# GpSimd's state-space tables in the written order and a step ahead, phasors with scratch of their own, a third modulation buffer, later first slabs of layer 1

## The chip, the cores and the metric

One core of a Trainium2 chip runs the whole program. The metric is device time in microseconds (us), the median of several executions. TensorE does the matrix products, VectorE, ScalarE and GpSimd the elementwise work, and SyncE issues nearly all transfers, in the order of its queue. In the views these are PE, DVE, ACT, POOL and SP (SPq where the queue itself is meant).

## The reference

A trunk of two layers on x (1024 positions by 1024 features, float32). Each layer normalises x, scales and shifts it by a modulation that is computed from a conditioning vector c, runs a mixer, and adds the gated result back:

```
mod = c @ mod_w[layer] + mod_b[layer]        # shift, scale, gate
h   = rms_norm(x, norm_w[layer]) * (1 + scale) + shift
x   = x + gate * mixer(h)
```

Layer 0's mixer projects h to five pieces. Two feed a causal convolution of 31 taps with a LayerNorm and SiLU behind it. One, u, feeds a diagonal complex state-space recurrence in 32 groups of 16 channels with 64 states each (x_t = a x_(t-1) + B u_t, y = Re(C x) + D u), with a GELU and a gated linear unit behind it. Both results are gated, joined and projected back. Layer 1's mixer is a dilated sliding-window attention with 24 heads in three patterns.

## The kernel before

Every float32 product is made of three products of a rounded high and a low part (`mm3`, L229 to L233; `split`, L202 to L212, makes the parts: the high part on ScalarE, the low part on VectorE or GpSimd). A weight piece arrives raw (`wr`, `wrp`, `wrg`, `fr`), is split into `wh` and `wl` (or `whp`, `wlp`, `whg`, `wlg`), and is used for 24 matmuls of 512 columns in each half of the sequence.

Layer 0 is a loop over *steps* t: 42 steps of two halves per weight piece, then 21 steps for the output projection, of which the last eight, p0 to p7, are t = 55 to 62. A table `side`, filled by `at(t, function)`, hangs small work onto the steps: the state-space part, the convolution, LayerNorm, the modulation of layer 1. The work of a step is issued ahead of the step's own matmuls. On VectorE, ScalarE and TensorE the instructions of layer 0 run in the order in which the program writes them (`manual_schedule`, L487). A scheduler that ranks by priority decides the order on GpSimd and on SyncE's queue. Each engine runs its own list strictly in order.

The state-space part runs in four *quarters* j of eight groups (`ssm_quarter`), one generator each, whose parts are hung at t = 4j + 2, 3, 5, 6, 7, 7, 8 and 11. At 4j + 2 come the phasors T (three VectorE instructions, then three on ScalarE; their scratch is TS), seven GpSimd instructions that make the table HC (scratch HT), four small copies into `bbd`, the 16 small matmuls `pk` that read HC and bbd, and a round trip through memory that makes the matrix M. At 4j + 3 come six GpSimd instructions that make G0 and G1 (scratch GS) and their transposes `pgt`; at 4j + 5 the matmuls sr and si, the rotations V and W by T and a scan W; behind that X, the output matmuls `py` and a round trip of Y. HT, G0, G1, GS and TS share one pool of three buffers, "t2". HC has two buffers, and `py` of a quarter is the last to read its HC.

The modulation rows of layer 1 (`mod_rows`) take 64 chunks of weights of 256 KB, two for each of 32 steps, into the two halves of a buffer `mw`; the matmuls are `pr`.

In LayerNorm `ln_center` makes squares `lq`, `ln_var` sums them by the matmul `va` (L598), `ln_rsqrt` and `ln_norm` follow.

At the end `residual` adds the projected half to x (`xr` loaded, x written, squares `xq`), `hidden` makes the first operands h of layer 1, and `first_slabs` (hung at t = 58 as `open_slabs`) loads four weight slabs `fr` of layer 1 and splits them, the low parts on GpSimd. fr uses the pool tag "cv", which has five buffers and is also that of xr, xq and rs.

Of the kernel before, what the change touches and what calls it, by code (L numbers as in the profile page):

```python
# [9 lines left out]
F32 = mybir.dt.float32  # L10
F32R = mybir.dt.float32r
I32 = mybir.dt.int32
AF = mybir.ActivationFunctionType
ALU = mybir.AluOpType
# [5 lines left out]
MAGIC = 12582912.0  # L20
NEG = -1e30
TURN = 6.2831845
# [43 lines left out]
MODR = ((0, 16), (0, 20), (1, 8), (1, 12), (1, 0), (1, 4), (1, 16), (1, 20))  # L66


class Trunk:
# [181 lines left out]
    def mod_rows(self, ps, pr):  # L251

        nc = self.nc
        w = self.u("mw", tag="mw").rearrange("p (i m n) -> p i m n", i=2, m=4)
        crep = self.cb[:, 0:256].rearrange("p (k n) -> p k n", k=8)
        rows = self.cb[:, 256:384]
        p = pr("pr")[:, 0:128]
        for n, (layer, m) in enumerate(MODR):
            for q in range(4):
                for i in range(2):  # L260
                    nc.sync.dma_start(w[:, i], self.I["mod_r"][n, 2 * q + i])
                yield
                for i in range(2):
                    k = 2 * q + i
                    for j in range(4):
                        nc.tensor.matmul(p[32 * j:32 * j + 32], lhsT=crep[:, k], rhs=w[:, i, j], start=(k == 0),  # L266
                                         stop=(k == 7), tile_position=(0, 32 * j))
            nc.scalar.activation(rows, p, AF.Copy)
            self.mod_late = (ps, rows, layer, m)

# [17 lines left out]
    def layer0(self):  # L288
        nc, tc, I = self.nc, self.tc, self.I
        with self.cx0 as cx:  # L290
# [6 lines left out]
            def ps(name, shape=None, tag="ps"):  # L297
                return pp.tile(shape or [128, 512], F32, tag=tag, name=name, bufs={"ps": 3, "pm": 2}[tag])
# [7 lines left out]
            def pc(name):  # L306
                return pp.tile([128, 2, 512], F32, tag="pc", name=name, bufs=1)
# [34 lines left out]
            with tc.tile_pool(name="start", bufs=8) as sp, order:  # L342
# [102 lines left out]
                sh = pc("sh")  # L445
# [35 lines left out]
                for j in (15, 4):  # L481
# [3 lines left out]
            nc.vector.tensor_copy(self.cb[:, 0:256].rearrange("p (k n) -> p k n", k=8),  # L485
                                  self.ccol.unsqueeze(2).to_broadcast([128, 8, 32]))
            cx.enter_context(tc.manual_schedule(engines={mybir.EngineType.DVE, mybir.EngineType.Activation,  # L487
                                                         mybir.EngineType.PE}))


            seq = [15]
# [45 lines left out]
            def at(t, fn, *a):  # L537
                side.setdefault(t, []).append(lambda: fn(*a))
# [2 lines left out]
            conv = [None] * 4  # L541
            at(1, self.rope_tables)
            for j in range(4):
                for t in (2, 3, 5, 6, 7, 7, 8, 11):
                    at(4 * j + t, next, quarter[j], None)
                for t in (8, 9, 10, 12):
                    at(4 * j + t, lambda j: next(conv[j], None), j)
# [62 lines left out]
            for b in range(2):  # L610
                at(25, ln_sum, b)
                t = 27 + 4 * b
                at(t, ln_mean, b)
                at(t, ln_center, b, 0)
                at(t + 1, ln_center, b, 1)
                at(t + 2, ln_var, b)
                at(t + 2, ln_rsqrt, b)
                at(t + 3, ln_norm, b, (0, 1, 2, 3))


            yc = [[None, None] for _ in range(8)]
# [24 lines left out]
            for n in range(8):  # L646
                b, j = divmod(n, 4)
# [39 lines left out]
            for t in range(42):  # L687
                i, h = divmod(t, 2)
# [10 lines left out]
                p = ps(f"p{key}_{h}")  # L699
# [4 lines left out]
                n = len(rh)  # L704
# [51 lines left out]

            for k in range(8):
                at(57 + k // 2, hidden, k)
            at(58, open_slabs)
            done, po = None, {}  # L760
            for i in range(21, len(seq)):
                t, key = i + 21, seq[i]
                m, b = int(key[1]), int(key[0] == "p")
# [24 lines left out]
    def first_slabs(self):  # L788

        nc = self.nc  # L790
        self.w1 = self.ctx.enter_context(self.tc.tile_pool(name="w1", bufs=4, side="right", reuse_waits="tile"))
        self.slabs = {}
        with self.prio(-150000):
            for i in range(4):
                raw = self.u(f"fr{i}", shape=[128, 2, 384], tag="cv")
                nc.sync.dma_start(raw, self.I["wqkv"][0, 0, :, 2 * i:2 * i + 2])
                self.slabs[0, i] = tuple(self.w1.tile([128, 2, 384], F32R, tag=t, name=t) for t in ("wh", "wl"))
                self.split(*self.slabs[0, i], raw, leng="gpsimd")
# [732 lines left out]
    def ssm_quarter(self, j, us, ps, ysg):  # L1531

        nc, S = self.nc, self.S

        def L(name, tag, shape, bufs=1):
            return self.sp.tile(shape, F32, tag=tag, name=name, bufs=bufs)

        gp, v = nc.gpsimd, nc.vector
        qs = slice(4 * j, 4 * j + 4)

        T = L(f"T{j}", "T", [128, 2, 4, 128], 2)
        n = L(f"TS{j}", "t2", [128, 4, 128], 3)
        sh = [128, 4, 128]
        y = T[:, 0]
        v.tensor_tensor(y, self.P["chunk"].unsqueeze(1).to_broadcast(sh), self.t8[:, qs].unsqueeze(2).to_broadcast(sh),
                        op=ALU.mult)
        v.tensor_scalar(n, y, MAGIC, None, ALU.add)
        v.scalar_tensor_tensor(n, n, MAGIC, y, ALU.subtract, ALU.subtract)
        nc.scalar.activation(T[:, 1], n, AF.Sin, scale=-TURN)
        nc.scalar.activation(y, n, AF.Abs)  # L1550
        nc.scalar.activation(y, y, AF.Sin, scale=-TURN, bias=self.quarter)

        sh = [128, 4, 8, 16]
        HC = L(f"HC{j}", "HC", [128, 2, 4, 8, 16], 2)
        tt = L(f"HT{j}", "t2", sh, 3)
# [13 lines left out]
        for i, b in enumerate((self.bbr, self.bbi)):  # L1569
            gp.tensor_copy(bd[0:64, :, i, 0:16], b[0:64, qs])  # L1570
            gp.tensor_copy(bd[64:128, :, i, 16:32], b[64:128, qs])
        pk = ps(f"pk{j}", [128, 128])
        for q in range(4):
            for i in range(2):
                nc.tensor.matmul(pk[32 * q:32 * q + 32], lhsT=bd[:, q, i],
                                 rhs=HC[:, i, q].rearrange("p t h -> p (t h)"), start=(i == 0), stop=(i == 1),
# [8 lines left out]
        for t in range(8):  # L1585
            nc.sync.dma_start(M[t::8], kd[:, :, (7 - t) * 16:(7 - t) * 16 + 128])
        yield

        sh = [128, 4, 16, 8]
        GT = L(f"GT{j}", "GT", [128, 2, 4, 128])  # L1590
        G = [L(f"G{j}{i}", "t2", sh, 3) for i in range(2)]
        tg = L(f"GS{j}", "t2", sh, 3)
        br = self.bbr[:, qs].unsqueeze(3).to_broadcast(sh)
        bi = self.bbi[:, qs].unsqueeze(3).to_broadcast(sh)
        pr7 = self.prr.rearrange("p t g -> p g t")[:, qs].unsqueeze(2).to_broadcast(sh)
        pi7 = self.pir.rearrange("p t g -> p g t")[:, qs].unsqueeze(2).to_broadcast(sh)
        gp.tensor_tensor(G[0], br, pr7, op=ALU.mult)
        gp.tensor_tensor(tg, bi, pi7, op=ALU.mult)
        gp.tensor_tensor(G[0], G[0], tg, op=ALU.subtract)
        gp.tensor_tensor(G[1], br, pi7, op=ALU.mult)  # L1600
        gp.tensor_tensor(tg, bi, pr7, op=ALU.mult)
        gp.tensor_tensor(G[1], G[1], tg, op=ALU.add)
        for i in range(2):
            pg = ps(f"pgt{j}{i}")
            for q in range(4):
                nc.tensor.transpose(pg[:, q * 128:(q + 1) * 128], G[i][:, q].rearrange("p h t -> p (h t)"),
                                    self.ident)
            nc.scalar.activation(GT[:, i], pg.rearrange("p (q n) -> p q n", q=4), AF.Copy)
        yield

        U = us[j]
        sr, si = ps(f"sr{j}"), ps(f"si{j}")
        for g in range(8):
            q, o = g // 2, 64 * (g % 2)
            for i, s in enumerate((sr, si)):
                nc.tensor.matmul(s[o:o + 64, q * 128:(q + 1) * 128], lhsT=GT[:, i, q, o:o + 64], rhs=U[:, g],
                                 start=True, stop=True)
        V = L(f"V{j}", "VW", [128, 2, 4, 128], 2)
        W = L(f"W{j}", "VW", [128, 2, 4, 128], 2)
        c, s = T[:, 0], T[:, 1]  # L1620
        r4 = lambda a: a.rearrange("p (q n) -> p q n", q=4)
# [10 lines left out]
                                     V[:, i, q], 0.0, ALU.mult, ALU.add)  # L1632
        yield
        X = L(f"X{j}", "X", [128, 2, 4, 128])
        gp.memset(X[:, :, :, 0:1], 0.0)
        xs = X[:, :, :, 1:128]
        V, W, c, s = V[:, :, :, 0:127], W[:, :, :, 0:127], c[:, :, 0:127], s[:, :, 0:127]
        v.tensor_tensor(xs[:, 0], W[:, 0], c, op=ALU.mult)
# [9 lines left out]
        for q in range(4):  # L1648
# [3 lines left out]
            for i in range(2):  # L1652
                for b in range(2):
                    o = 64 * b
                    nc.tensor.matmul(d[b], lhsT=HC[o:o + 64, i, q].rearrange("p t h -> p (t h)"),
                                     rhs=X[o:o + 64, i, q], start=False, stop=(i == 1))
# [12 lines left out]
def p_order():  # L1669

    p = np.arange(1024)
    tok = p // 512 * 512 + p // 32 % 4 * 128 + p % 32 * 4 + p // 128 % 4
    n = np.arange(128)
    return tok, n % 32 * 4 + n // 32


def lay_out(inp):
    a = {k: np.asarray(v) for k, v in inp.items()}
    f = np.float32
    tok, loc = p_order()  # L1680
    col = lambda v: np.ascontiguousarray(v.reshape(-1, 128).T)
    pair = lambda v: v.reshape(16, 2, 64, -1).transpose(1, 2, 0, 3).reshape(128, -1)
# [37 lines left out]
    taps = np.zeros((512, 54), f)  # L1720
    taps[:, 7:38] = a["conv_dw_w"][0].T[:, ::-1]
    taps = np.stack([taps[:, 7 - t:47 - t] for t in range(8)], 1)
    w = a["attn_w_in"][0].reshape(8, 128, 10240)
    qkv = w[:, :, :9216].reshape(8, 128, 3, 3, 8, 128).transpose(4, 3, 1, 0, 2, 5)
    pos = a["positions"][0]
    post = pos[tok].reshape(8, 128).T
    tl = lambda w: w.reshape(w.shape[0] // 128, 128, -1, 128).transpose(2, 1, 0, 3)
# [46 lines left out]
```

## Time and profile before

| what | before |
|---|---|
| median of 3 executions | 1764.66 us |
| lowest, highest | 1764.46, 1767.72 us |
| the profiled execution's own time | 1767.46 us |
| its span in the profile | 1765.7 us |
| TensorE busy | 1675.6 us, 95% |
| VectorE, ScalarE, GpSimd busy | 937.0, 618.7, 505.3 us |
| mean granted clock of TensorE | 0.974 |

The span runs from the first to the last instruction; the execution's own time holds some 1.8 us more around it. Layer 0 takes about the first 560 us. TensorE is the busiest engine, so what counts is where it stands still, and where its clock is granted below full speed (1 in the views).

### The profile page before, as it was taken

What the parts mean: (1) busy time and instruction counts of PE and PEld (TensorE: products, weight loads), DVE (VectorE), ACT (ScalarE), POOL (GpSimd) and SP (SyncE); (2) the same over time, 40 slices, a digit from 0 to 9 for tenths busy, and PEclk for the clock granted to TensorE, in tenths of its full rate; (3) what the DMA queues carried; (4) which work ended last, traced back from release to release, by engine and by line L of the source; (5) the groups of instructions that cost most, each with busy time, mean ns of one, the idle gap of its engine ahead of it and who ended that gap; (6) DMA issues with size and microseconds to landing.
All of it is one profiled execution on the core that took longest, in us unless ns stands there. A gap on an engine that the chain in (4) does not pass through costs nothing.

```text
span 1765.7 us, 28609 instructions
## 1 busy us (share of the span) xinstructions
PE 1675.6 (95%) x10520; PEld 1524.2 (86%) x10520; DVE 937.0 (53%) x2332; ACT 618.7 (35%) x1860; POOL 505.3 (29%) x737
## 2 busy tenths in 40 slices
PE   8967779989997999999999999999999999999999
PEld 5755657767776999999999999999999999999887
DVE  8823444344555745654664564565575475465551
ACT  5311322363333433333333333333333333333410
POOL 6234320200014532332332233233233243333000
PEclk8988889999998999999999999999999999999999
DMA  9433445524553201211311211211221221121243
GB/s 353 143 95 90 135 144 160 174 96 138 183 177 98 62 25 55 73 43 41 87 43 35 65 62 29 76 52 34 61 76 34 58 82 37 44 63 61 84 156 102
DMA packets 94189, 159.84 MB, mean 91 GB/s; under 512 B 13281, under 2 KB 43745, under 8 KB 94050
## 3 DMA queue, kind: packets, MB, share of 16 engines
q1 hardware_dynamic: 94050, 158.02, 29.1%
q8 instruction: 83, 1.36, 0.3%
q14 instruction: 56, 0.46, 0.1%
HBM read 130.54 MB, written 23.23 MB: 87 GB/s over the span
## 4 chain that ended last, share of the span: by engine, by line
PE 84%; issue 5%; DVE 3%; POOL 3%; ACT 2%; DMA 1%; SPq 0%; POOLq 0%; ACTq 0%; DVEq 0%
PE pj L233 17%; PE pj L231 17%; PE pj L232 17%; PE O L1142 4%; PE S L1093 4%; PE p L231 4%; PE p L232 3%; PE p L233 3%; PE tqk L1047 2%; PE tP L1120 2%; PE po L233 2%; PE po L231 2%; PE po L232 2%; PE pr L266 1%; DMA mw<-in_mod_r 1%
## 5 line engine op out<-in xcount | busy, mean ns | idle before, releaser
L231 PE MATMUL pj<-wh,h 128*128 128x384 f32 x1536 | 542.9, 353 | 0.0
L233 PE MATMUL pj<-wh,h 128*128 128x384 f32 x1536 | 516.7, 336 | 0.8 <-DVE h L224 0.8
L232 PE MATMUL pj<-wl,h 128*128 128x384 f32 x1536 | 516.0, 336 | 0.0
L231 PEld LDWEIGHTS pj<-wh,h 128*128 128x128 f32 x1536 | 289.1, 188 | 1.1 <-issue 0.2
L232 PEld LDWEIGHTS pj<-wl,h 128*128 128x128 f32 x1536 | 289.7, 189 | 0.3 <-issue 0.2
L233 PEld LDWEIGHTS pj<-wh,h 128*128 128x128 f32 x1536 | 288.3, 188 | 1.4 <-DVE h L224 1.4
L1032 POOL TENSOR_TENSOR B<-u,sin 128x256 f32<-128x256 f32 x192 | 190.3, 991 | 210.6 <-DVE u L1028 210.6
L1004 ACT ACTIVATE sq<-pj 128x128 f32<-128x128 f32 x384 | 103.0, 273 | 351.1 <-PE pj L233 321.2
L212 DVE TENSOR_TENSOR wl<-raw,wh 128x768 fp32r<-128x768 f32 (+1 forms) x124 | 115.9, 949 | 124.5 <-ACT wh L209 123.9
L1005 POOL TENSOR_SCALAR ss<-ss 128x2 f32<-128x2 f32 x192 | 40.8, 212 | 488.4 <-ACT sq L1004 488.2
L1028 DVE SCALAR_TENSOR_TENSOR u<-pj,ss,pk 128x128 f32<-128x128 f32 x384 | 116.3, 344 | 74.7 <-POOL ss L1006 74.6
L1069 DVE COPY qk<-tqk 128x256 f32<-128x256 f32 x188 | 79.0, 420 | 139.5 <-PE tqk L1047 139.5
L1006 POOL TENSOR_TENSOR ss<-ss,mh 128x2 f32<-128x2 f32 x192 | 138.1, 719 | 16.0
L1113 ACT ACTIVATE E<-E,nm 128x256 f32<-128x256 f32 (+2 forms) x128 | 71.3, 557 | 198.7 <-DVE nm L1112 198.7
L231 PE MATMUL p<-h0h,wh 128*128 128x512 f32 x272 | 114.8, 422 | 0.0
L232 PE MATMUL p<-h0l,wh 128*128 128x512 f32 x272 | 110.6, 407 | 0.0
L233 PE MATMUL p<-h0h,wl 128*128 128x512 f32 x272 | 110.0, 404 | 0.0
L209 ACT ACTIVATE wh<-raw 128x768 fp32r<-128x768 f32 (+1 forms) x124 | 97.3, 790 | 28.8 <-PE po L232 15.0
L1040 DVE TENSOR_TENSOR u<-A,B 128x128 f32<-128x128 f32 x192 | 56.2, 293 | 88.4 <-POOL B L1032 81.6
L1039 DVE TENSOR_TENSOR A<-u,cos 128x256 f32<-128x256 f32 x192 | 96.6, 503 | 4.4
L1093 PE MATMUL S<-qk 128*128 128x128 f32 x544 | 86.4, 274 | 0.0
L1093 PEld LDWEIGHTS S<-qk 128*128 128x128 f32 x544 | 80.9, 190 | 1.3
(449 smaller groups left out, 2789.2 us busy)
## 6 DMA issues: line engine op xcount, KB each, us to landing
raw<-in_wqkv SPq DMA_DIRECT2D x92, 384.0 KB
mw<-in_mod_r SPq DMA_DIRECT2D x64, 256.0 KB
wr<-in_w SPq DMA_DIRECT2D x17, 512.0 KB
al<-ad SPq DMA_DIRECT2D x16, 512.0 KB
x<-in_x SPq DMA_DIRECT2D x8, 512.0 KB
mw<-in_scale SPq DMA_DIRECT2D x8, 512.0 KB
mw<-in_shift SPq DMA_DIRECT2D x8, 512.0 KB
xr<-in_xp SPq DMA_DIRECT2D x16, 256.0 KB
```

Source lines behind the costliest of these rows:

```text
L209: nc.scalar.activation(hi, src, AF.Copy)
L212: getattr(nc, leng).tensor_tensor(lo, src, hi.bitcast(F32), op=ALU.subtract)
L231: mm(ps, lhsT=lh, rhs=rh, start=first, stop=False)
L232: mm(ps, lhsT=lh, rhs=rl, start=False, stop=False)
L233: mm(ps, lhsT=ll, rhs=rh, start=False, stop=last)
L1004: sc.activation(sq[:, i], p[:, i * 128:(i + 1) * 128], AF.Square, accum_out=ss[:, i:i + 1])
L1006: gp.tensor_tensor(ss, ss, mh, op=ALU.pow)
L1028: v.scalar_tensor_tensor(u[:, i].rearrange("p a b -> p (a b)"), p[:, i * 128:(i + 1) * 128], ss[:, i:i + 1], w, ALU.mult, ALU.mult)
L1032: gp.tensor_tensor(f(B), f(u), sin[:, ti].unsqueeze(1).to_broadcast([128, 4, 64]), op=ALU.mult)
L1039: v.tensor_tensor(f(A), f(u), cos[:, ti].unsqueeze(1).to_broadcast([128, 4, 64]), op=ALU.mult)
L1069: v.tensor_copy(out, tp)
L1093: pe.matmul(ps[:, i * 128:(i + 1) * 128], lhsT=qT[h, g, t], rhs=kT[h, g, kt], start=True, stop=True)
```

## The change

GpSimd joins the engines in written order. In `ssm_quarter` the tables HC, bbd and G become a first part of their own, at t = 0, 3, 8 and 12; pk, its round trip and M stay at 4j + 2, the transposes at 4j + 3; the phasors move to 4j + 4, and their scratch TS to another pool ("e"). `mod_rows` takes half of the tile cb as a third buffer and asks for chunk c + 3 right behind the matmuls of chunk c. LayerNorm's `ln_var`, `ln_rsqrt` and `ln_norm` come a step later. `open_slabs` moves from t = 58 to 60, and fr from the tag "cv" to the default one. X's small memset moves from GpSimd to VectorE.

```diff
 def mod_rows(self, ps, pr):
     w = self.u("mw", tag="mw").rearrange("p (i m n) -> p i m n", i=2, m=4)
+    w = [w[:, 0], w[:, 1], self.cb[:, 512:1024].rearrange("p (m n) -> p m n", m=4)]
+    def load(c):
+        if c < 8 * len(MODR):
+            nc.sync.dma_start(w[c % 3], self.I["mod_r"][c // 8, c % 8])
+    for c in range(3):
+        load(c)
...
         for q in range(4):
-            for i in range(2):
-                nc.sync.dma_start(w[:, i], self.I["mod_r"][n, 2 * q + i])
             yield
-            for i in range(2):
-                k = 2 * q + i
+            for k in (2 * q, 2 * q + 1):
+                c = 8 * n + k
                 for j in range(4):
-                    nc.tensor.matmul(..., rhs=w[:, i, j], ...)
+                    nc.tensor.matmul(..., rhs=w[c % 3][:, j], ...)
+                load(c + 3)
...
 cx.enter_context(tc.manual_schedule(engines={mybir.EngineType.DVE, mybir.EngineType.Activation,
-                                             mybir.EngineType.PE}))
+                                             mybir.EngineType.PE, mybir.EngineType.Pool}))
...
 for j in range(4):
-    for t in (2, 3, 5, 6, 7, 7, 8, 11):
+    for t in ((0, -1, 0, 0)[j], 2, 3, 4, 5, 6, 7, 7, 8, 11):
         at(4 * j + t, next, quarter[j], None)
...
-    at(t + 2, ln_var, b)
-    at(t + 2, ln_rsqrt, b)
-    at(t + 3, ln_norm, b, (0, 1, 2, 3))
+    at(t + 3, ln_var, b)
+    at(t + 3, ln_rsqrt, b)
+    at(t + 4, ln_norm, b, (0, 1, 2, 3))
...
-at(58, open_slabs)
+at(60, open_slabs)
...
-    raw = self.u(f"fr{i}", shape=[128, 2, 384], tag="cv")
+    raw = self.u(f"fr{i}", shape=[128, 2, 384])
...
 def ssm_quarter(...):
-    (T: scratch TS from "t2"; three VectorE, three ScalarE instructions)
     (HC: seven GpSimd instructions; bbd: four copies)
+    (G0, G1: six GpSimd instructions)
+    yield
     (pk, kp, Kd, M)
     yield
-    (G0, G1: six GpSimd instructions)
     (pgt, GT)
+    yield
+    (T: scratch TS from self.ep, tag "e"; the same six instructions)
     yield
...
-    gp.memset(X[:, :, :, 0:1], 0.0)
+    v.memset(X[:, :, :, 0:1], 0.0)
```

(The lines in parentheses stand for code that is moved unchanged but for the scratch.)

In the order of GpSimd's instructions in quarter 0, in the stretch that ends the table HC, stood before (HC_902, HT_903 and G_964, GS_966 are the tables and scratch of this quarter, 0):

```order
L1561 TENSOR_TENSOR HT_903<-pk,pi 128x512
L1597 TENSOR_TENSOR G_964<-bbr,prr 128x512
L1562 TENSOR_TENSOR HC_902<-HC_902,HT_903 128x512
L1598 TENSOR_TENSOR GS_966<-bbi,pir 128x512
L1564 TENSOR_TENSOR HT_903<-pk,pr 128x512
L1599 TENSOR_TENSOR G_964<-G_964,GS_966 128x512
L1565 TENSOR_TENSOR HC_902<-HC_902,HT_903 128x512
L1601 TENSOR_TENSOR GS_966<-bbi,prr 128x512
L1566 TENSOR_SCALAR HC_902<-HC_902 128x512
L1600 TENSOR_TENSOR G_965<-bbr,pir 128x512
```

and now, from the start of the same quarter's tables:

```order
L1555 TENSOR_TENSOR HC_813<-pk,pr 128x512
L1556 TENSOR_TENSOR HT_814<-pk,pi 128x512
L1557 TENSOR_TENSOR HC_813<-HC_813,HT_814 128x512
L1558 TENSOR_TENSOR HC_813<-pk,pi 128x512
L1559 TENSOR_TENSOR HT_814<-pk,pr 128x512
L1560 TENSOR_TENSOR HC_813<-HC_813,HT_814 128x512
L1561 TENSOR_SCALAR HC_813<-HC_813 128x512
L1565 COPY bbd_781<-bbr 64x4x16
L1566 COPY bbd_781<-bbr 64x4x16
L1565 COPY bbd_781<-bbi 64x4x16
L1566 COPY bbd_781<-bbi 64x4x16
L1575 TENSOR_TENSOR G_826<-bbr,prr 128x512
```

The two tables were interleaved, with GS, which takes a buffer of "t2", ahead of the last three instructions of HC; now HC's seven instructions and the copies stand together, and all of G behind them.

In ScalarE's order at the end of layer 0 (wh<-fr are the high parts of layer 1's slabs, xq the squares of a residual, whp the high part of an output-projection piece, h an operand of layer 1) stood before:

```order
L218 ACTIVATE h_3_0_4065<-x_2_0_3749,mod_0_2847 128x512
L209 ACTIVATE wh<-fr_4075 128x768
L209 ACTIVATE wh<-fr_4081 128x768
L209 ACTIVATE wh<-fr_4087 128x768
L209 ACTIVATE wh<-fr_4093 128x768
L732 ACTIVATE xq_4127<-x_2_1_4049 128x512
L209 ACTIVATE whp_4131<-wrp_3973 128x1024
```

and now:

```order
L218 ACTIVATE h_6_0_4152<-x_6_0_3877,mod_4_3195 128x512
L218 ACTIVATE h_7_0_4156<-x_6_0_3877,mod_4_3195 128x512
L209 ACTIVATE wh<-fr_4166 128x768
L209 ACTIVATE wh<-fr_4172 128x768
L209 ACTIVATE wh<-fr_4178 128x768
L209 ACTIVATE wh<-fr_4184 128x768
L739 ACTIVATE xq_4218<-x_4_1_4142 128x512
L209 ACTIVATE whp_4222<-wrp_4059 128x1024
```

The four slab splits stood ahead of the whp that p5 reads; now they stand ahead of the whp that p7 reads, behind h6 and h7.

## Rows read from the trace of the kernel before

**Rows 1.** Stretches: length; busy PE, PEld, DVE, ACT, POOL; clock; DMA; GB/s.
```profile
72.00:140.00 68.00, 41.47 (x221) 32.23 (x219) 26.16 (x39) 17.39 (x25) 25.84 (x25) 0.81 0.47 147
590.00:1000.00 410.00, 410.00 (x2575) 402.15 (x2574) 224.90 (x655) 149.27 (x569) 135.63 (x214) 1.00 0.19 52
```

**Rows 2.** TensorE's waits, 72 to 600: total us, times, longest.
```profile
PE pk L1575 <- POOL HC L1566: 47.1, 4, 15.1
PE pr L266 <- DMA mw<-in_mod_r: 11.0, 8, 3.2
PE pop L231 <- ACT whp L209: 10.2, 2, 9.4
PE va L598 <- DVE lq L592: 6.0, 3, 3.6
```

**Rows 3.** GpSimd's waits, 66 to 340: total us, times, longest.
```profile
POOL GS L1598 <- ACT T L1550: 76.7, 4, 22.7
...
POOL HC L1560 <- PE py L1655: 34.3, 2, 18.2
```

**Rows 4.** Timeline, GpSimd, quarter 0: start, duration, instruction, wait ahead.
```profile
66.11 1.61 POOL L1560 TENSOR_TENSOR HC<-pk,pr 128x512 f32<-128x512 f32 x1 [24.27 <-ACT h0h L407]
...
69.20 2.09 POOL L1560 TENSOR_TENSOR HC<-pk,pr 128x512 f32<-128x512 f32 x1
...
91.58 1.31 POOL L1598 TENSOR_TENSOR GS<-bbi,pir 128x512 f32<-128x512 f32 x1 [13.70 <-ACT T L1550]
92.85 1.10 POOL L1564 TENSOR_TENSOR HT<-pk,pr 128x512 f32<-128x512 f32 x1
...
97.62 1.50 POOL L1566 TENSOR_SCALAR HC<-HC 128x512 f32<-128x512 f32 x1
```

**Rows 5.** Chain that ended last, quarters 1 and 2: start, duration, piece.
```profile
130.33 1.28 DVE W L1631 x4
...
133.49 0.63 ACT T L1549
...
163.53 0.65 PE py L1655 x8
```

**Rows 6.** Stretches of single steps, columns as in group 1.
```profile
100.20:107.60 7.40, 7.40 (x27) 5.92 (x25) 0.53 (x2) 0.00 (x0) 2.38 (x6) 0.74 0.29 66
153.40:159.00 5.60, 5.60 (x28) 4.56 (x25) 0.00 (x0) 1.54 (x3) 0.00 (x0) 1.00 0.30 97
252.20:258.80 6.60, 6.60 (x27) 5.30 (x25) 6.59 (x11) 0.00 (x0) 2.03 (x2) 0.84 0.35 98
285.00:292.30 7.30, 7.30 (x28) 5.61 (x24) 1.54 (x5) 0.07 (x1) 0.00 (x0) 0.77 0.44 146
538.10:547.50 9.40, 9.32 (x26) 6.64 (x26) 5.71 (x7) 3.58 (x5) 2.40 (x2) 0.66 0.47 149
```

**Rows 7.** Timeline, SyncE's queue, quarter 1: issue time, its length.
```profile
163.56 5.04 SPq L1586 DMA_DIRECT2D M<-Kd  x8
168.71 5.23 SPq L1660 DMA_DIRECT2D Yd<-Y  x8
```

**Rows 8.** Timeline, TensorE: a chunk of modulation weights, and pk of quarter 2.
```profile
176.87 0.43 PE L266 MATMUL pr<-mw,cb 128*32 128x128 f32 x8 [1.76 <-DMA mw<-in_mod_r]
...
195.49 0.67 PE L1575 MATMUL pk<-HC,bbd 128*32 128x128 f32 x8 [9.12 <-POOL HC L1566]
```

**Rows 9.** Timeline, VectorE: one form beside GpSimd and alone.
```profile
68.19 4.17 DVE L212 TENSOR_TENSOR wl<-wr,wh 128x1024 fp32r<-128x1024 f32 x2
...
87.31 1.22 DVE L212 TENSOR_TENSOR wl<-wr,wh 128x1024 fp32r<-128x1024 f32 x1 [2.67 <-ACT wh L209]
```

**Rows 10.** Timeline, VectorE, end of layer 0.
```profile
544.08 0.74 DVE L726 SCALAR_TENSOR_TENSOR x<-pop,mod,xr 128x512 f32<-128x512 f32 x1
...
551.53 0.74 DVE L726 SCALAR_TENSOR_TENSOR x<-pop,mod,xr 128x512 f32<-128x512 f32 x1
```

**Rows 11.** Timeline, ScalarE, end of layer 0.
```profile
534.16 0.84 ACT L209 ACTIVATE wh<-fr 128x768 fp32r<-128x768 f32 x1 [4.46 <-DMA fr<-in_wqkv]
```

More of the change, by code (lines that the diff above doesn't have):

```diff
@@ L259, in mod_rows @@
             for q in range(4):
-                for i in range(2):
-                    nc.sync.dma_start(w[:, i], self.I["mod_r"][n, 2 * q + i])
                 yield
-                for i in range(2):
-                    k = 2 * q + i
+                for k in (2 * q, 2 * q + 1):
+                    c = 8 * n + k
                     for j in range(4):
-                        nc.tensor.matmul(p[32 * j:32 * j + 32], lhsT=crep[:, k], rhs=w[:, i, j], start=(k == 0),
+                        nc.tensor.matmul(p[32 * j:32 * j + 32], lhsT=crep[:, k], rhs=w[c % 3][:, j], start=(k == 0),
                                          stop=(k == 7), tile_position=(0, 32 * j))
+                    load(c + 3)
             nc.scalar.activation(rows, p, AF.Copy)
@@ L1539, in ssm_quarter @@
         qs = slice(4 * j, 4 * j + 4)
[L1541 to L1551, printed above, removed]
         sh = [128, 4, 8, 16]
@@ L1571, in ssm_quarter @@
             gp.tensor_copy(bd[64:128, :, i, 16:32], b[64:128, qs])
+        sh = [128, 4, 16, 8]
+        G = [L(f"G{j}{i}", "t2", sh, 3) for i in range(2)]
+        tg = L(f"GS{j}", "t2", sh, 3)
+        br = self.bbr[:, qs].unsqueeze(3).to_broadcast(sh)
+        bi = self.bbi[:, qs].unsqueeze(3).to_broadcast(sh)
+        pr7 = self.prr.rearrange("p t g -> p g t")[:, qs].unsqueeze(2).to_broadcast(sh)
+        pi7 = self.pir.rearrange("p t g -> p g t")[:, qs].unsqueeze(2).to_broadcast(sh)
+        gp.tensor_tensor(G[0], br, pr7, op=ALU.mult)
+        gp.tensor_tensor(tg, bi, pi7, op=ALU.mult)
+        gp.tensor_tensor(G[0], G[0], tg, op=ALU.subtract)
+        gp.tensor_tensor(G[1], br, pi7, op=ALU.mult)
+        gp.tensor_tensor(tg, bi, pr7, op=ALU.mult)
+        gp.tensor_tensor(G[1], G[1], tg, op=ALU.add)
+        yield
         pk = ps(f"pk{j}", [128, 128])
@@ L1587, in ssm_quarter @@
         yield
-        sh = [128, 4, 16, 8]
         GT = L(f"GT{j}", "GT", [128, 2, 4, 128])
[L1591 to L1602, printed above, removed]
         for i in range(2):
@@ L1608, in ssm_quarter @@
             nc.scalar.activation(GT[:, i], pg.rearrange("p (q n) -> p q n", q=4), AF.Copy)
+        yield
+        T = L(f"T{j}", "T", [128, 2, 4, 128], 2)
+        n = self.ep.tile([128, 512], F32, tag="e", name=f"TS{j}").rearrange("p (q n) -> p q n", q=4)
+        sh = [128, 4, 128]
+        y = T[:, 0]
+        v.tensor_tensor(y, self.P["chunk"].unsqueeze(1).to_broadcast(sh), self.t8[:, qs].unsqueeze(2).to_broadcast(sh),
+                        op=ALU.mult)
+        v.tensor_scalar(n, y, MAGIC, None, ALU.add)
+        v.scalar_tensor_tensor(n, n, MAGIC, y, ALU.subtract, ALU.subtract)
+        nc.scalar.activation(T[:, 1], n, AF.Sin, scale=-TURN)
+        nc.scalar.activation(y, n, AF.Abs)
+        nc.scalar.activation(y, y, AF.Sin, scale=-TURN, bias=self.quarter)
         yield
```

## The prediction

> **What bounds the kernel now.** I read the stretches first. In layer 1 TensorE is busy for all 410.00 of 410 us at clock 1.00; in the first stretch of the state-space quarters it is busy for 41.47 of 68.00 at 0.81 [rows 1]. So this change, which is all in layer 0, can only win there. The list of TensorE's waits says what for: pk, which waits for GpSimd's last HC instruction, 47.1 us in four waits; the modulation matmuls pr, which wait for their weights, 11.0 in eight; an output-projection piece, 10.2; LayerNorm's va, 6.0 [rows 2].
>
> GpSimd itself is not short of time. Its own waits hold 76.7 us ahead of GS, for the ScalarE instruction on the phasors T [rows 3]: GS takes a buffer of "t2" that TS held. The timeline shows it in quarter 0: GS starts at 91.58 after 13.70 us of idling, and HC ends at 99.12 [rows 4], which is when pk can begin. In quarter 1 the chain goes one link further back: T comes behind the W scan on VectorE and ends at 134.1 [rows 5]. Thus T, which nobody needs for three more steps, delays HC, which TensorE needs at once.
>
> A wait costs more than itself. The step right behind pk runs 7.40 us at clock 0.74 in quarter 0 and 6.60 at 0.84 in quarter 3, where an undisturbed one takes 5.60 at 1.00 [rows 6]. That is between the chip's two levels, 1.2 and 2.4 GHz: the step starts low after TensorE stood still and ends high.
>
> **The tables.** Per quarter thirteen GpSimd instructions and four small copies are moved ahead of pk, as the order shows; none is added. What goes is the wait, 47.1 [rows 2], and the slow steps behind it: 7.40 and 6.60 for the first and last, 1.8 and 1.0 over 5.60; the two others I take as like these, in sum 2 x (1.8 + 1.0) = 5.6 [rows 6]. Together 52.7.
>
> Is HC in time everywhere? Quarter 0: HC starts at 66.11. Seven instructions at the 1.61 seen there end at 77.4, at 2.09, the longest seen, at 80.7 [rows 4], and the copies add at most about 1. TensorE arrives at pk 15.1 before 99.2, at 84.1 [rows 2, 4]. Quarters 2 and 3: HC may only be written when py of two quarters before has read its buffer. Before, py of quarter 0 ended at 164.2 [rows 5] and TensorE reached pk of quarter 2 at 195.49 - 9.12 = 186.4 [rows 8]; 22 us less what other waits go in between (1.76 there) still leaves some 19 for 7 x 1.5 + 1 = 11.5, or 15.6 at 2.09. Margins are thus 2 to 8 us. G, the transposes and T have a step and more each. T's six instructions now precede sr, si and V by one step of 5.6 us and more; they take 0.63 to 0.7 us each, some 4, and the slack pays. X's memset on VectorE lies in the time that it waits.
>
> Here the order of engines could hurt. With GpSimd busy, VectorE's split of 128 x 1024 took 4.17 us for two, 2.09 each, with GpSimd idle 1.22 [rows 9]; GpSimd's own instruction took 2.09 against 1.10 [rows 4]. The Trainium skill, "GPSIMD Engine Reference", section 1 (Specifications), says that GpSimd shares its SBUF interfaces with VectorE and that VectorE's instructions with two SBUF inputs contend; the trace agrees (2.09 against 1.10). If every one of the thirteen ran at 2.09, the tables would take 27 us a quarter and VectorE's work beside them 1.7 times its time. VectorE is busy for 26.16 of 68 [rows 1], so the sum is left as it is, and the contention raises the chance of the first rival.
>
> **The modulation weights.** SyncE's queue is in order. In quarter 1, M's eight transfers took 5.04 us to issue and Y's eight 5.23 [rows 7]; the pair of chunks behind them landed late, and pr waited 1.76 for the first [rows 8]. With three buffers the first chunk of a step is asked for a step earlier than now; the second still has one step's lead, since its buffer is free only when the first of the step before has been used. I take half of 11.0, 5.5. Bounds: 3, if the second chunk is what is mostly late; 11.0 and a slow step behind it, 7.30 against 5.60 [rows 6], together 12.7.
>
> **LayerNorm.** va waits 6.0 in three waits, at most 3.6 [rows 2]. A step later is 2.8 us for a half-length step (the gated unit's pieces have half the matmuls) and 5.6 for a full one. I take all 6.0; at worst 4; at best 6.0 and a slow step's 1.7 more [rows 6]. Its consumers, the output projection's operands, come many steps on.
>
> **The slabs.** Now: 10.2 of waiting and a step of 9.40 where 5.60 would do [rows 2, 6], 14.0 in all. It comes from ScalarE, which waited 4.46 for fr ahead of whp [rows 11]; xr stood behind fr in the shared buffers. After: the chain from one residual to the next takes 551.53 - 544.08 = 7.45 on VectorE [rows 10] where TensorE wants 5.60, so p5 and p6 wait 1.85 each, 3.7; and p7's whp now stands behind four wh of 0.84, 3.4 [rows 11], with a slow step, half of the 3.8 above, behind it. The gain is 14.0 - 3.7 - 3.4 - 1.9 = 5.0. Bounds: 0.5 with fr again 4.46 late; 10.6 if the residuals keep up and p7's step stays fast.
>
> **Sum.** 52.7 + 5.5 + 6.0 + 5.0 = 69.2 us. The profiled execution took 1767.46, so the same one would take 1698.3; it stands 2.8 above the median, 1764.66, from which the forecast follows: 1695.5.
>
> **Rivals.** First: HC is still late in quarters 2 and 3, where it follows py and contends with VectorE. For it: 34.3 us of GpSimd's waits are already for py [rows 3], and the margin at 2.09 is 3 us or less. Against: at 1.5 each it is 7. If 9.1 stays in both, with the slow step of 1.0 behind, 20.2 come back: 1716.
>
> Second, on the slower side: SyncE's queue becomes the bound. The loads are now 64 single ones; each waits for the matmuls of the chunk three before, and M, Y, the layer's weights wr and the convolution's reads stand behind it. The waits for pk, which covered such lateness, are gone. For it: pr waits at all, behind 10.3 us of issues [rows 7, 8]. The Trainium skill, "DMA: Bandwidth & Descriptors", section "Anatomy of one DMA — SWDGE (gpsimd) path", says that a transfer's semaphore wait happens on the issuing sequencer before dispatch; by that, everything behind such a load is late with it, and the trace, where pr waits behind Y's issues, agrees so far. It decides from 69.2 / 32 = 2.2 us for each of the 32 modulation steps; at 2.5 each it costs 80 and the time is 1775. Against: the matmuls that a load waits for take 0.43 us for eight [rows 8], just ahead of the step's own 5.60.
>
> Third: T was not what held GS, and pk's wait stays whole, released by something else, such as the transposes that free "t2". Then only the small terms count, 16.5: 1748. Against: the row of GS itself names T's second ScalarE instruction as its releaser, and so does the list for all four quarters [rows 3, 4].
>
> Fourth: the end of layer 0 gives nothing or loses 3, as p7 waits for all four slabs: up to 8 back, 1703, within the range below.
>
> **Chances.** Forecast with its small terms anywhere in their bounds 0.66; first rival 0.19; slabs 0.07; third 0.03; queue 0.03; else, about evenly on both sides, 0.02. The range: best terms 52.7 + 12.7 + 7.7 + 10.6 = 83.7 give 1681, the first rival 1716. A measurement of this kernel tells some 0.2%, 3.5 us, from no change: every case but the queue is beyond it on the faster side. So faster 0.96, the same 0.01, slower 0.03.
>
> **What would show it.** Right: no wait of pk on HC; GpSimd's first wait of a quarter for py or pgt, not for T; clock 1.00 in the steps behind pk; pr's waits halved; va's gone; waits of 1 to 5 us at p5 to p7. Wrong: pk still waiting, with HC's instructions at 2 us; SyncE's M or wr issued behind a modulation load with TensorE waiting for either; a new wait for T's consumers V and W.

## The result and the profile after

The changed kernel takes 1700.06 us, median of 4 executions (1699.71 to 1702.04), against 1765.06 before in the same comparison: a ratio of 0.9631, 95% interval 0.9615 to 0.9648, or 65.0 us less. The forecast was 1695.5 (69.2 less) with a range of 1681 to 1716. The profiled execution took 1702.04 us with a span of 1700.3, at a mean granted clock of 0.991 (0.974 before).

Where the time went is read from five starts in TensorE's timeline: the first projection matmul p, the first matmul pg of the gated linear unit, the first of the output projection (poo0b), the first statistic st inside it, and layer 1's first, pj.

| stretch | before | after | change | forecast |
|---|---|---|---|---|
| p (72.39; 72.03) to pg: state space, convolution, modulation | 287.34 | 231.34 | -56.0 | -58.2 |
| pg (359.73; 303.37) to poo0b: gated unit, LayerNorm, gates | 92.17 | 85.97 | -6.2 | -6.0 |
| poo0b (451.90; 389.34) to st | 52.82 | 52.72 | -0.1 | 0 |
| st (504.72; 442.06) to pj: end of layer 0 | 55.67 | 53.07 | -2.6 | -5.0 |
| pj (560.39; 495.13) to the end: layer 1 | 1205.3 | 1205.2 | -0.1 | 0 |

The first line is the forecast's sum of the tables (52.7) and the modulation weights (5.5). Layer 1 has not moved, so all of it was won in the places that the profile of before named.

TensorE's waits of the changed kernel, 60 to 600 us (total us, times, longest), which answer to [rows 2]:

```profile
PE pop L231 <- ACT whp L209: 4.7, 3, 3.7
PE pgt L1602 <- DVE kp L1589: 4.5, 1, 4.5
PE pr L272 <- DMA mw<-in_mod_r: 4.5, 5, 1.4
PE pop L233 <- DVE wlp L212: 4.0, 4, 2.5
PE va L605 <- DVE lq L599: 3.0, 1, 3.0
PE pr L272 <- DMA cb<-in_mod_r: 1.7, 1, 1.7
```

No wait of pk is left of the 47.1. In its place is one that the forecast did not have: the transposes pgt, 4.5 us, for the VectorE instruction kp. pr is down from 11.0 to 6.2 (4.5 + 1.7), va from 6.0 to 3.0. The end of layer 0 (pop) waits 4.7 + 4.0.

GpSimd's waits, 60 to 340, which answer to [rows 3]:

```profile
POOL ls L585 <- PE pc L830: 78.8, 1, 78.8
POOL HC L1555 <- PE py L1664: 48.2, 2, 26.6
POOL HC L1555 <- ACT h0h L414: 26.4, 1, 26.4
POOL ls L585 <- DVE cv L854: 12.9, 1, 12.9
```

It no longer waits for T at all (ls belongs to the convolution's LayerNorm). HC waits for py, 48.2 us in two waits, as the prediction said it would, and TensorE does not wait for it in turn.

Two stretches as in [rows 1], and two pieces behind waits, as in [rows 6] (the columns are those of group 1):

```profile
72.00:140.00 68.00, 63.46 (x399) 50.25 (x398) 44.03 (x55) 23.51 (x34) 40.15 (x34) 0.95 0.58 179
590.00:1000.00 410.00, 410.00 (x2575) 402.16 (x2574) 233.26 (x667) 148.24 (x568) 136.03 (x213) 1.00 0.19 55
95.50:101.30 5.80, 5.80 (x18) 4.63 (x17) 0.00 (x0) 0.60 (x1) 5.39 (x8) 0.60 0.84 247
190.97:198.30 7.33, 7.33 (x28) 5.56 (x24) 4.16 (x5) 0.13 (x1) 6.51 (x5) 0.77 0.46 165
```

TensorE is busy for 63.46 us of the stretch where it was for 41.47, at clock 0.95 where it was 0.81. The slow steps behind pk are gone. Others stand behind the waits that are left: 0.60 right behind the new wait of pgt, and a step of 7.33 at 0.77 behind a wait of pr.

### The profile page after: what moved, and what is told of

Same layout as the page of the kernel before. It is cut to its first block, busy times and chain, and to the rows that moved or that the text cites. A ratio compares the mean times of both kernels' runs of the same rounds, so it can differ in the third digit from the quotient of the medians.

```text
span 1700.3 us, 28611 instructions
## 1 busy us (share of the span) xinstructions
PE 1663.6 (98%) x10520; PEld 1516.7 (89%) x10520; DVE 952.2 (56%) x2336; ACT 618.9 (36%) x1860; POOL 514.6 (30%) x733
## 4 chain that ended last, share of the span: by engine, by line
PE 83%; issue 5%; DVE 4%; DMA 3%; ACT 2%; SPq 2%; POOL 1%; ACTq 0%; DVEq 0%; POOLq 0%
PE pj L231 17%; PE pj L233 17%; PE pj L232 17%; PE O L1149 4%; PE S L1100 4%; PE p L231 3%; PE p L232 3%; PE p L233 3%; PE tqk L1054 2%; PE tP L1127 2%; PE po L233 2%; PE po L232 2%; PE po L231 2%; DMA mw<-in_mod_r 1%; SPq L1669 1%
```

## The experiments

All are edits of the changed kernel, except where the text says that they are edits of the kernel before. "..." in a diff marks lines that are left out.

**1. The scratch alone.** The kernel before, with TS from the pool of temporaries:

```diff
-        n = L(f"TS{j}", "t2", [128, 4, 128], 3)
+        n = self.ep.tile([128, 512], F32, tag="e", name=f"TS{j}").rearrange("p (q n) -> p q n", q=4)
```

> The kernel before with one edit: the phasors' scratch TS comes from the pool of temporaries instead of the three shared buffers; GpSimd's order stays the scheduler's, and T stays ahead of pk. Theory (the shared buffer was the whole cause of the wait of pk): GS no longer waits for T, pk's waits fall from 47.1 us to under 5, and the time from 1765 to about 1712. Rival (the order of GpSimd is needed too, because G's instructions stand between HC's): half or more of pk's wait stays, 1735 to 1750.

Measured: 1724.9 us (ratio 0.9774, 0.9759 to 0.9788), 40 less with one line. TensorE's waits:

```profile
PE pr L266 <- DMA mw<-in_mod_r: 12.6, 13, 1.8
...
PE pgt L1606 <- DVE kp L1579: 4.1, 1, 4.1
PE pk L1575 <- POOL HC L1566: 3.6, 1, 3.6
```

The wait for pk falls from 47.1 to 3.6, in quarter 0 only. So the shared buffer was its cause, as the theory has it; the time is 13 over the theory's 1712. Waits make up 9.3 of it: pk's 3.6, 4.1 of pgt that it had not waited before, and pr's 12.6 instead of 11.0. Slow steps stand behind all three.

**2. The state-space edit alone.** The kernel before with the whole edit of `ssm_quarter` and its steps (tables first, T later, own scratch), the scheduler still ordering GpSimd:

```diff
-                for t in (2, 3, 5, 6, 7, 7, 8, 11):
+                for t in ((0, -1, 0, 0)[j], 2, 3, 4, 5, 6, 7, 7, 8, 11):
...
```

> The kernel before with the state-space edit alone: the tables as a step of their own, the phasors later and with their own scratch, X's memset on VectorE; the scheduler still orders GpSimd, and modulation, LayerNorm and slabs are as before. Theory (the shared scratch was the cause, the tables' own step is worth nothing more): 1722 to 1727, as with the scratch alone, 1724.9. Rival (the own step removes something besides the wait for T): 1716 to 1720, which is also what comes out if the effects of the other parts, 11, 4 and 3.5 us as measured in the changed kernel, are added to its time with the scheduler's order, 1699.7.

Measured: 1718.45 (0.9740, 0.9726 to 0.9753), in the rival's range: 6.5 less than with the scratch alone, so the moved steps do more than free T's buffer, which this run's theory denied. pk still waits 3.6 here. VectorE's timeline in quarter 0, with the scratch alone:

```profile
93.52 1.62 DVE L212 TENSOR_TENSOR wl<-wr,wh 128x1024 fp32r<-128x1024 f32 x1 [2.67 <-ACT wh L209]
95.06 1.59 DVE L1545 TENSOR_TENSOR T<-pk,t 128x512 f32<-128x512 f32 x1
...
99.69 0.28 DVE L1579 COPY kp<-pk 128x128 f32<-128x128 f32 x1
```

and with the whole state-space edit:

```profile
93.47 1.61 DVE L212 TENSOR_TENSOR wl<-wr,wh 128x1024 fp32r<-128x1024 f32 x1 [2.67 <-ACT wh L209]
95.00 0.28 DVE L1582 COPY kp<-pk 128x128 f32<-128x128 f32 x1
```

With the scratch alone, T's three instructions (the first is shown) stand ahead of kp, which empties pk's accumulator; it comes at 99.69 and the transposes wait for it. With T two steps later kp comes at 95.00, and pgt waits nowhere. That is the 4.1 us and the slow step behind it (8.01 us where an undisturbed one, timed from its first matmul to its last, takes 5.86).

**3. GpSimd's order left to the scheduler.**

```diff
-                                                         mybir.EngineType.PE, mybir.EngineType.Pool}))
+                                                         mybir.EngineType.PE}))
```

> The changed kernel, with GpSimd's order left to the scheduler again; the tables' own step, T's place and its scratch stay. Theory (the written order adds little once TS has its own scratch): GpSimd's list has G's and the next HC's instructions between those of HC, some five of 1.5 to 2 us in quarter 0, so pk waits about 3 us there and little elsewhere: 1700 to 1705. Rival (the written order carries the gain): pk waits 5 to 10 us in each quarter, 1720 to 1745.

Measured: 1699.67 (0.9632, 0.9618 to 0.9647), no difference from 1700.06. But the waits differ:

```profile
PE pk L1585 <- POOL HC L1561: 3.6, 1, 3.6
...
PE pgt L1602 <- DVE kp L1589: 0.2, 1, 0.2
```

pk waits its 3.6 again, as the theory says, and of pgt's 4.5 only 0.2 is left: kp comes at 95.0 us here and at 94.3 in the changed kernel, so TensorE waits for it at the transposes or has waited at pk already. The written order won time that the next late instruction took back.

**4. Two modulation buffers again** (the loop of the kernel before in `mod_rows`, pairs of loads).

> The changed kernel, with the modulation weights asked for in pairs into two buffers again. Theory (the third buffer takes the wait off the first chunk of a step and leaves it on the second): pr's waits go from 6.2 us back to 10 to 12, some slow steps return, the time is 1705 to 1708. Rival (the waits come from the place of the loads in SyncE's queue behind the transfers of M and Y, whatever the number of buffers): pr's waits stay within 1.5 us of 6.2 and the time within 2 us of 1700.

Measured: 1711.24 (0.9695, 0.9679 to 0.9712), 11 more than with three, where the theory gave 5 to 8.

```profile
PE pr L266 <- DMA mw<-in_mod_r: 13.0, 13, 2.0
```

pr waits 13.0, not 6.2, and in TensorE's timeline three steps of 7.41 us, against 5.87 undisturbed, stand behind these waits where the changed kernel has one.

**5. The third buffer alone**, in the kernel before.

> The kernel before with the three modulation buffers alone. Theory (the waits for pk, which stay here, had hidden part of the lateness of the loads, so that the buffer is worth more behind them): the gain is 4 to 7 us, pr's waits 11.0 fall to about 5, 1758 to 1761. Rival (the buffer is worth the same with and without the waits for pk): 11 us as in the changed kernel, 1753 to 1755.

Measured: 1755.69 (0.9953, 0.9939 to 0.9967), 9.4 less. TensorE's waits:

```profile
PE pk L1582 <- POOL HC L1573: 47.1, 4, 15.1
...
PE pr L272 <- DMA cb<-in_mod_r: 1.9, 2, 1.6
...
PE pr L272 <- DMA mw<-in_mod_r: 1.6, 2, 1.1
```

pr falls from 11.0 to 3.5 (1.9 + 1.6) while pk keeps its 47.1. The value lies between theory and rival and nearer to the rival, and the 1.8 between it and the 11.2 of experiment 4 is less than this measurement tells from no change. That the waits for pk hid part of the loads' lateness is thus not shown.

**6. LayerNorm a step earlier again.**

```diff
-                at(t + 3, ln_var, b)
+                at(t + 2, ln_var, b)
...
```

> The changed kernel, with LayerNorm's variance, root and scaling a step earlier again. Theory (the later step is worth the waits of va that it took away): va waits 6.0 us again instead of 3.0, and the time is 1704 to 1706, since the step behind and the root on TensorE's path come back as well. Rival (the waits only moved to other matmuls): the time is within 2 us of 1700.

Measured: 1704.28 (0.9657, 0.9638 to 0.9676), 4.2 more, by the theory, with va's waits back:

```profile
PE va L605 <- DVE lq L599: 6.0, 3, 3.6
```

**7. The slabs at their old place.**

```diff
-            at(60, open_slabs)
+            at(58, open_slabs)
...
-                raw = self.u(f"fr{i}", shape=[128, 2, 384])
+                raw = self.u(f"fr{i}", shape=[128, 2, 384], tag="cv")
```

> The changed kernel, with the four first slabs back at step 58 and in the buffers shared with the residuals' rows. Theory (the whole slab edit is worth what the end of layer 0 shows, 2.6 us): a wait of some 9 us at p5 comes back and those at p6 and p7 fall; the time is 1702 to 1704. Rival (GpSimd's written order has changed what the slabs wait for, so the old place costs more now): p5 waits over 12 us, 1706 or more.

Measured: 1703.54 (0.9651, 0.9633 to 0.9668), 3.5 more, as the theory said, though that is no more than this measurement tells from no change; the returned wait is the firmer sign. One wait is longer than it foresaw and the later ones are shorter:

```profile
PE pop L231 <- ACT whp L209: 11.9, 2, 11.1
...
PE pop L233 <- DVE wlp L212: 1.0, 2, 0.5
```

**8. The slabs a step later still**, behind the split of the piece that p7 reads.

```diff
-            at(60, open_slabs)
+            at(61, open_slabs)
```

> The changed kernel, with the four first slabs at step 61 instead of 60, so that their splits stand behind the split of the piece that p7 reads. Theory (p7's wait of 3.7 and 2.5 us and its slow step come from the four slab splits ahead of it on ScalarE and from GpSimd's slab parts beside VectorE's): p7 waits as p6 does, 1.3 in all, layer 1 starts 5 to 7 us earlier, and the time is 1693 to 1695. Rival (the slabs are then late for layer 1): the first projections wait 3 us or more for them and the time is 1697 to 1701.

Measured: 1693.05 (0.9590, 0.9572 to 0.9607), 7.0 less, the theory's 5 to 7.

```profile
PE pop L233 <- DVE wlp L212: 2.1, 4, 0.5
...
PE pop L231 <- ACT whp L209: 1.6, 2, 0.8
```

The longest wait of p7 is gone (3.7 and 2.5 before this edit), and layer 1 takes no longer for it: 1205.3 us.

**9. The rotary tables at step 19**, in temporaries.

```diff
-            at(1, self.rope_tables)
...
+            at(19, self.rope_tables)
...
-        xn = self.u("ro", shape=[128, 2, 8, 64], tag="mw")
-        x, n = xn[:, 0], xn[:, 1]
+        x, n = (self.ep.tile([128, 8, 64], F32, tag="e", name=f"ro{i}") for i in range(2))
```

> The changed kernel, with the rotary tables (fourteen VectorE and two ScalarE instructions, from step 1) moved to step 19 and into temporaries. Theory (the new 4.5 us wait of the second transposes in quarter 0 is VectorE still at these tables when pk's evacuation kp is due, and GpSimd beside it): that wait goes, no other of its size comes, and the time falls from 1700 to 1695 or 1696. Rival (kp is late for ScalarE's wh and VectorE's wl ahead of it, not for the tables): 2 to 4 us of the wait stay, 1698 to 1700; or the tables stall a later step and the time stays.

Measured: 1693.36 (0.9595, 0.9579 to 0.9611), 6.7 less, more than the theory's 4 to 5. VectorE in quarter 0 of the changed kernel (ro is a rotary table, wl the split ahead of kp):

```profile
79.58 0.43 DVE L174 TENSOR_SCALAR ro<-ro 128x512 f32<-128x512 f32 x1
...
85.28 1.49 DVE L177 TENSOR_SCALAR ro<-ro 128x512 f32<-128x512 f32 x1
...
92.59 1.82 DVE L212 TENSOR_TENSOR wl<-wr,wh 128x1024 fp32r<-128x1024 f32 x1 [2.61 <-ACT wh L209]
94.33 0.28 DVE L1589 COPY kp<-pk 128x128 f32<-128x128 f32 x1
```

and with the tables moved:

```profile
84.13 2.29 DVE L212 TENSOR_TENSOR wl<-wr,wh 128x1024 fp32r<-128x1024 f32 x1 [10.88 <-ACT wh L209]
86.34 0.28 DVE L1588 COPY kp<-pk 128x128 f32<-128x128 f32 x1
```

kp comes 8.0 us earlier, no wait of pgt is left, and no slow piece behind it; that piece explains why the gain is 2 more than the 4.5 of the wait. How the tables hold kp back is seen on ScalarE in the changed kernel:

```profile
88.58 0.63 ACT L184 ACTIVATE ro<-ro 128x512 f32<-128x512 f32 x1 [12.94 <-DVE ro L182]
...
91.50 1.06 ACT L209 ACTIVATE wh<-wr 128x1024 fp32r<-128x1024 f32 x1
```

ScalarE's first instruction of the rotary tables waits 12.94 us for VectorE's, and wh stands behind it in ScalarE's order. VectorE then waits 2.61 us for wh ahead of wl, and kp stands behind wl. So the late wh, which the rival names, is a link of the theory's chain and not another cause.

**10. The modulation loads ahead on SyncE's queue.**

```diff
-                nc.sync.dma_start(w[c % 3], self.I["mod_r"][c // 8, c % 8])
+                with self.prio(-180000):
+                    nc.sync.dma_start(w[c % 3], self.I["mod_r"][c // 8, c % 8])
```

> The changed kernel, with the modulation loads given priority on SyncE's queue, so that they stand between the second and third of M's eight transfers, ahead of Y's, and ahead of the convolution's; buffers and transfers are the same. Theory (pr waits because M's and Y's issues, ten microseconds, stand ahead of the load): pr's waits fall from 6.2 us to under 1, with the one slow step behind them, and the time to 1692 to 1694. Rival (the load is late since its buffer is free only a step before, or the transfer itself is slow): pr's waits stay over 4 and the time within 2 us of 1700; or M and Y are now late, and py or the rotations wait.

Measured: 1694.40 (0.9602, 0.9581 to 0.9623), 5.7 less, 0.4 short of the theory's range; no wait of pr is in the list of waits any more. SyncE's queue in the changed kernel, at the place of [rows 7]:

```profile
135.72 5.04 SPq L1596 DMA_DIRECT2D M<-Kd  x8
140.86 5.05 SPq L1669 DMA_DIRECT2D Yd<-Y  x8
146.01 0.85 SPq L259 DMA_DIRECT2D mw<-in_mod_r  x2
```

and here:

```profile
134.07 1.19 SPq L1597 DMA_DIRECT2D M<-Kd  x2
135.35 1.01 SPq L260 DMA_DIRECT2D mw<-in_mod_r  x2
136.41 3.75 SPq L1597 DMA_DIRECT2D M<-Kd  x6
140.26 4.85 SPq L1670 DMA_DIRECT2D Yd<-Y  x8
```

The loads of the changed kernel are issued at 146.01, behind sixteen transfers of M and Y; the second chunk lands late, and TensorE waits 1.10 us for it at 148.72. Here they are issued at 135.35. The number of buffers says how early a load may be asked for; the queue says when it is.

**11. All three further edits together** (8, 9 and 10).

> The changed kernel with the rotary tables at step 19, the slabs at step 61 and the modulation loads ahead on SyncE's queue, together. Theory (the three waits lie at different places and none hides another): the effects 6.7, 7.0 and 5.7 add, 1680 to 1683; TensorE waits for pk, pgt and pr nowhere. Rival (one hides part of another, as the waits for pk had hidden those for the modulation weights): 1685 to 1689, with a new wait in place of one removed.

Measured: 1678.26 (0.9520, 0.9507 to 0.9533), 21.8 less than the changed kernel, where 19.4 was the sum of the three (the 2.4 beyond it is less than this measurement tells from no change); the fastest kernel here. pk and pgt wait nowhere, pr 0.7 us in all. TensorE's longest waits, and the stretch of [rows 1]:

```profile
PE va L606 <- DVE lq L600: 3.0, 1, 3.0
PE pop L231 <- ACT whp L209: 2.2, 3, 0.8
PE pop L233 <- DVE wlp L212: 2.1, 4, 0.5
PE poo3b L231 <- ACT who3a L209: 1.3, 1, 1.3
```

```profile
72.00:140.00 68.00, 68.00 (x531) 54.43 (x533) 32.27 (x45) 21.61 (x32) 43.96 (x42) 1.00 0.62 189
```

TensorE is now busy for all of that stretch at clock 1.00.

**12. The same with the scheduler's order on GpSimd.**

> The kernel with all three further edits, with GpSimd's order left to the scheduler. Theory (the written order does save pk's wait of 3.6 us in quarter 0, but in the changed kernel the late evacuation kp takes the same time back at the transposes; with the rotary tables gone from there the order shows its worth): pk waits 2 to 4 us again with a slow step of 1 to 2 behind it, 1681 to 1684 against 1678.3. Rival (the written order is worth nothing anywhere, since GpSimd without the rotary tables beside it is fast enough either way): within 2 us of 1678.

Measured: 1680.59 (0.9513, 0.9500 to 0.9526), 2.3 more, with single times of 1679.21 to 1681.50 against 1677.55 to 1682.34. That is under what this measurement tells from no change, and the two ratios to the kernel before, 0.9513 and 0.9520, lie the other way round.

```profile
PE pk L1585 <- POOL HC L1561: 0.8, 1, 0.8
```

Neither text has it: pk waits, but 0.8 us and not 2 to 4. With no rotary tables on VectorE beside it GpSimd's instructions of the tables take 1.1 to 1.5 us between 74 and 86 us, so that even the interleaved order is nearly in time.

## Why the prediction was right, and where its terms were off

**The tables, 52.7.** The mechanism was right: T's scratch held GpSimd up, GpSimd held pk up, and experiment 1 shows the link by itself. The whole state-space edit alone measured 46.7 (1765.1 - 1718.45), 6 short: there the scheduler's order leaves pk's wait of 3.6 with a slow step behind it, and pr waits 12.8 instead of 11.0. The step that was off in the changed kernel reads "G, the transposes and T have a step and more each": true for G, but the transposes also need the accumulator that pk used, and kp, which frees it, comes late on VectorE, behind a split that is held up by the rotary tables (experiment 9). The wait of 15.1 for pk had covered that. In the changed kernel it costs 4.5 at pgt and some 2 in the piece at clock 0.60 behind it, which experiment 9 takes away together. The slow steps were priced rightly: the four behind pk took 7.63, 7.81, 6.91 and 6.79 us in the kernel before, 5.7 over four of 5.86, where the prediction has 5.6.

**HC in time.** Right: no wait of pk in any quarter. The last copy ends 3.7 us ahead of pk in quarter 0, where 2 were named at the least, and 10 and 12 ahead in quarters 2 and 3, more than was named. GpSimd ran at up to 2.10 us in quarter 0, so the first rival's contention was there, without the price that it needed. The Trainium skill, "GPSIMD Engine Reference", section 1 (Specifications), names contention with VectorE's instructions in a two-port mode or with two SBUF inputs; the traces agree (2.10 us beside VectorE's split, which has two inputs, against 1.10), and show that VectorE pays too (below).

**The modulation weights, 5.5.** Too low: 9.4 alone, 11.2 in the changed kernel. The half that was taken for the second chunk was too much, and the slow steps behind the waits, which stood only in the upper bound of 12.7, belonged in the sum. The queue's place in it was right: experiment 10.

**LayerNorm, 6.0.** 6.2 in the stretch, 4.2 by taking the edit back; the last wait, 3.0, stayed, so "all 6.0" was half right as a wait. The rest of the 6.2 is a wait of mc for ScalarE, 1.0, that went as well, and steps that ran slow behind the waits; that the sum came out at the forecast is luck.

**The slabs, 5.0.** 2.6 to 3.5. p5 and p6 waited 0.7 and 1.35, less than the 1.85 each that was priced, p7 more than the 3.4: whp came behind four slab splits of ScalarE, and then wlp, made from it on VectorE, ran slowly beside GpSimd's slab parts. ScalarE and VectorE at p7, and VectorE there in experiment 8:

```profile
479.53 3.03 ACT L209 ACTIVATE wh<-fr 128x768 fp32r<-128x768 f32 x4
...
482.98 1.04 ACT L209 ACTIVATE whp<-wrp 128x1024 fp32r<-128x1024 f32 x1
```

```profile
484.87 2.82 DVE L212 TENSOR_TENSOR wlp<-wrp,whp 128x1024 fp32r<-128x1024 f32 x1
```

```profile
478.23 1.23 DVE L212 TENSOR_TENSOR wlp<-wrp,whp 128x1024 fp32r<-128x1024 f32 x1 [0.22 <-ACT whp L209]
```

wlp takes 2.82 us where it takes 1.23 with the slabs a step later. Together p7 lost 3.7 + 2.5 in waits and some 2 in a slow step. Experiment 8 takes both away at once; what ScalarE's order and the slow wlp cost singly was not tried.

**The rivals.** SyncE's queue did not become the bound; it costs the 5.7 of experiment 10, far from the 69 that would have decided. The third, that something else held GS, fell with experiment 1. The fourth came in part: p7 did wait for all four slabs, but the end of layer 0 still gained. GpSimd's written order itself, the change's first words, is worth nothing that can be measured here (experiments 3 and 12).

**The sum.** 69.2 was forecast and 65.0 measured. Taken singly, the state-space edit, the third buffer, LayerNorm and the slabs are worth 46.7, 9.4 to 11.2, 4.2 and 3.5, together 64 to 66. The tables were 6 short and the weights 4 to 6 over, so that the whole came nearer than its terms is in part luck.

## What to carry to other kernels

When a long wait is removed, list what else was late under its cover, and not only on the engine that was waited for: here it was the instruction that empties the accumulator, on a third engine. A scratch buffer shared by two chains orders them as hard as a semaphore does, and giving one chain its own was worth 40 of the 65 us. A further buffer lets a load be asked for earlier only as far as the queue that issues it gets to it; look at both.

## What the runs showed of the hardware that was not expected

A VectorE instruction slows down beside GpSimd, in these rows by a larger factor with one input in memory than with two. The table instructions of L173 to L183 with one input of 128 x 512 take 0.43 us with GpSimd idle (experiment 9, at 241 us) and 1.49 (L177 at 85.28) beside GpSimd's tables. The split of 128 x 1024 with two inputs takes 1.22 with GpSimd idle [rows 9], 1.82 in quarter 0 and 2.82 beside GpSimd's slab parts. It is not always VectorE that pays: in experiment 8 the split at 478.23 takes 1.23 beside GpSimd's part of h (L227, at 478.43), and that takes 2.18, where it takes 1.26 with VectorE idle (changed kernel, at 481.37). There the split started first, at 484.87 GpSimd did; whether that decides was not tried.

A wait is not always followed by a slow step: in the kernel before with the third buffer alone a wait of pr of 1.64 us has none behind it, in the changed kernel one of 1.72 has a step of 7.33 at clock 0.77. What decides between the two was not tried. Nor does the clock fall right behind the wait: in that step it is 1.00 from 190.97 to 192.20, 0.50 from 192.30 to 195.10, and 1.00 again from 195.90, while behind the 15.1 us wait for pk in the kernel before it is 0.50 from the first matmul.
